# Copies of two PSUM banks at a time, and a small early zero write to the output, in a batched fp32-in, fp32-out matmul

## The chip, the cores and the metric

The kernel runs on one core of one Trainium2 chip. The metric is the device time of one execution in microseconds (us); a comparison is made between executions of the two kernels on the same chip.

## The reference

Sixteen independent products: for each batch, x (768 x 512) transposed times y (768 x 1024).

```python
def setup_inputs():
    batch, m, k, n = 16, 512, 768, 1024
    return {
        "x": np.random.randn(batch, k, m).astype(np.float32),
        "y": np.random.randn(batch, k, n).astype(np.float32),
    }

def reference(x, y):
    return np.einsum('bkm,bkn->bmn', x, y).astype(np.float32)
```

## The kernel before

Each batch loads x (1.5 MB) and y (3 MB) as fp32, casts them to bf16 on the vector engine (DVE), and runs 48 matmuls of 512 columns on the tensor engine (PE): 4 row blocks x 2 column halves x 6 steps of the contraction. The 6 steps accumulate in one bank of PSUM, the memory that PE writes its results to, so a batch has eight groups in eight banks. The scalar engine (ACT) copies each bank to SBUF, the memory that loads and stores use, and one store writes the 2 MB of the batch. All loads and stores are issued from one queue, the sync queue (SP in the profile), and the store of a batch stands four batches of loads behind it.

```python
    psum = ctx.enter_context(tc.tile_pool(name="psum", bufs=8, space=bass.MemoryType.PSUM))
    LAG = 4
    ...
        for b in range(B):
            ...
            load(xs[:], x_v[b], 1)
            for h in range(halves):                  # 2 in the last batch, else 1
                ks = slice(h * KT // halves, (h + 1) * KT // halves)
                load(ys[:, ks], y_v[b, :, ks], 1)
            if b >= LAG:
                store(b - LAG)
            ...                                      # casts x_sb<-xs, y_sb<-ys on DVE
            for h in range(halves):
                for mo in range(MT):
                    for nt in range(NT):
                        if h == 0:
                            ps[mo, nt] = psum.tile([P, NF], FP32, name="ps")
                        for kt in range(h * KT // halves, (h + 1) * KT // halves):
                            mm(ps[mo, nt], x_w, y_sb, kt, mo, nt)
                        if h == halves - 1:
                            nc.scalar.copy(o_sb[:, mo, nt * NF:(nt + 1) * NF], ps[mo, nt][:])
        for b in sorted(o_tiles):
            store(b)
```

## Time and profile before

| | before |
|---|---|
| time, median of the runs beside the first measurement of the change | 262.25 us (262.04 to 262.52, 4 runs) |
| span of the profiled execution | 260.5 us |
| packets of the sync queue, share of the 16 DMA engines' span | 98.4% |
| bytes read and written | 109.06 MB, at a mean of 419 GB/s |
| busy: PE / DVE / ACT | 73% / 32% / 29% |
| copies out of PSUM | 128 of 587 ns |

The row to start from is the third. DMA engines that are busy for 98.4% of the span leave at most the other 1.6%, some 4 us, to be won by other engines, at the start and at the end. The table also says what can cost time: whatever is added to the DMA engines. The lines themselves stand in the prediction below.

In the windows view, GB/s divided by the DMA share is the rate at which the DMA engines move data while they are busy. It is about 430 where all packets take their usual time (430 / 1.01 = 426 from 10 to 55 us before), and falls where packets take longer.

### The profile page before, as it was taken

The page shows a single profiled execution, that of the slowest core. Times are in us where ns is not written, and L with a number is a line of the kernel's source. Part 1 is how long each engine was busy: PE and PEld are TensorE (multiplying, and loading weights), DVE is VectorE, ACT ScalarE, POOL GpSimd, SP SyncE. Part 2 cuts the span into 40 slices and gives each one's busy share as a digit, 9 for nine tenths or more (in the row PEclk, how much of TensorE's full clock was granted, in tenths as well). Part 3 has the DMA queues.
Part 4 walks back from the last instruction along what each step waited for, and adds up shares of the span by engine and source line. Part 5 has one row for each costly group of instructions (what it writes and reads, how often), then busy time and mean ns, then how long its engine had stood idle before and what let it go on. Part 6 is the DMA issues. An engine that isn't in the chain of part 4 may idle for free.

```text
span 260.5 us, 1879 instructions
## 1 busy us (share of the span) xinstructions
PE 191.3 (73%) x768; PEld 89.3 (34%) x768; DVE 83.1 (32%) x48; ACT 76.4 (29%) x129; POOL 0.2 (0%) x4
## 2 busy tenths in 40 slices
PE   0049999897939959688496966969789395899600
PEld 0014555453513514334142432434335142355200
DVE  0271633525222252322524214252132522252000
ACT  1003444442421403324032330323314043141600
POOL 0000000000000000000000000000000000000000
PEclk9999999999985977979898896797979889799955
DMA  7999999999999999999999999999999999999994
GB/s 279 434 434 411 445 423 436 426 387 420 446 416 442 423 422 455 409 440 418 438 435 415 453 418 431 423 428 449 410 443 421 426 445 407 431 430 430 435 428 201
DMA packets 7065, 109.18 MB, mean 419 GB/s; under 512 B 784, under 2 KB 784, under 8 KB 784
## 3 DMA queue, kind: packets, MB, share of 16 engines
q1 hardware_dynamic: 7056, 109.06, 98.4%
q8 instruction: 6, 0.10, 0.1%
q14 instruction: 3, 0.02, 0.0%
HBM read 75.50 MB, written 33.55 MB: 419 GB/s over the span
## 4 chain that ended last, share of the span: by engine, by line
DMA 74%; DVE 11%; PE 8%; issue 0%; ACT 0%; SPq 0%; DVEq 0%
DMA ys<-in_y_dram 74%; DVE y_sb L78 11%; PE ps L56 8%; ACT o_sb L93 0%; SPq L50 0%; DVEq L78 0%
## 5 line engine op out<-in xcount | busy, mean ns | idle before, releaser
L56 PE MATMUL ps<-y_sb,x_sb 128*128 128x512 bf16 x768 | 191.3, 412 | 53.8 <-DVE y_sb L78 53.8
L56 PEld LDWEIGHTS <-x_sb 128*128 128x128 bf16 x768 | 89.3, 118 | 155.2 <-issue 45.9
L93 ACT COPY o_sb<-ps 128x512 f32<-128x512 f32 x128 | 75.1, 587 | 168.6 <-PE ps L56 168.2
L78 DVE CAST y_sb<-ys 128x3072 bf16<-128x3072 f32 x32 | 55.0, 1757 | 87.4 <-DMA ys<-in_y_dram 87.4
L75 DVE CAST x_sb<-xs 128x3072 bf16<-128x3072 f32 x16 | 28.2, 1760 | 66.6 <-DMA xs<-in_x_dram 60.4
L93 ACT ACT_TABLE_LOAD x1 | 1.3, 1283 | 0.7 <-PEq L110 0.7
L110 POOL MEMSET const-bfloat16-1.0<- 128x1 bf16 x1 | 0.1, 101 | 0.0
L110 POOL MEMSET const-uint8-127<- 128x1 uint8 x1 | 0.1, 101 | 0.0
L110 POOL MEMSET const-float32-0.0<- 128x1 f32 x1 | 0.1, 98 | 0.2 <-issue 0.2
L110 POOL MEMSET const-float32-1.0<- 128x1 f32 x1 | 0.1, 98 | 0.0
## 6 DMA issues: line engine op xcount, KB each, us to landing
ys<-in_y_dram SPq DMA_DIRECT2D x15, 3072.0 KB, 28.1
out_dram<-o_sb SPq DMA_DIRECT2D x16, 2048.0 KB, 32.6
xs<-in_x_dram SPq DMA_DIRECT2D x16, 1536.0 KB, 29.7
ys<-in_y_dram SPq DMA_DIRECT2D x2, 1536.0 KB, 26.1
```

What stands on the lines that cost most here:

```text
L56: nc.tensor.matmul(ps[:], x_w[:, kt, mo], y_sb[:, kt, nt * NF:(nt + 1) * NF], start=(kt == 0), stop=(kt == KT - 1))
L75: nc.vector.tensor_copy(x_sb[:], xs[:])
L78: nc.vector.tensor_copy(y_sb[:, ks], ys[:, ks])
L93: nc.scalar.copy(o_sb[:, mo, nt * NF:(nt + 1) * NF], ps[mo, nt][:])
L110: nc = _bacc.Bacc("TRN2", target_bir_lowering=False, num_devices=1)
```

## The change

Two things are changed. PSUM tiles become two banks wide, so that ACT copies 1,024 columns with one instruction in place of twice 512 and pays ACT's fixed cost of an instruction once in place of twice. And a tile of zeros, 128 rows of 512 B, is written to the first output batch on the sync queue just behind the first loads; the store of batch 0 overwrites it later. The write may have been meant to ready the output's memory or the queue before the first real store comes.

```diff
-    psum = ctx.enter_context(tc.tile_pool(name="psum", bufs=8, space=bass.MemoryType.PSUM))
+    psum = ctx.enter_context(tc.tile_pool(name="psum", bufs=4, space=bass.MemoryType.PSUM))
+    z_pool = ctx.enter_context(tc.tile_pool(name="z_pool", bufs=1))
 ...
+            if b == 0:
+                z = z_pool.tile([P, 128], FP32, name="z")
+                nc.vector.memset(z[:], 0.0)
+                nc.sync.dma_start(o_v[0, :, 0, 0:128], z[:])
             if b >= LAG:
                 store(b - LAG)
 ...
                 for mo in range(MT):
+                    if h == 0:
+                        ps[mo] = psum.tile([P, NT, NF], FP32, name="ps")
                     for nt in range(NT):
-                        if h == 0:
-                            ps[mo, nt] = psum.tile([P, NF], FP32, name="ps")
                         for kt in range(h * KT // halves, (h + 1) * KT // halves):
-                            mm(ps[mo, nt], x_w, y_sb, kt, mo, nt)
-                        if h == halves - 1:
-                            nc.scalar.copy(o_sb[:, mo, nt * NF:(nt + 1) * NF], ps[mo, nt][:])
+                            nc.tensor.matmul(
+                                ps[mo][:, nt], x_w[:, kt, mo],
+                                y_sb[:, kt, nt * NF:(nt + 1) * NF],
+                                start=(kt == 0), stop=(kt == KT - 1))
+                    if h == halves - 1:
+                        nc.scalar.copy(o_sb[:, mo].rearrange("p (t f) -> p t f", f=NF), ps[mo][:])
```

The rest of the diff writes the helpers load, store and mm out in line and changes nothing in the instructions.

More of the change, by code (lines that the diff above doesn't have):

```diff
@@ L47 @@
     o_tiles = {}
-    def load(dst, src, rows):
-        nc.sync.dma_start(dst, src)
     def store(b):
-        nc.sync.dma_start(o_v[b], o_tiles.pop(b)[:])
-    def mm(ps, x_w, y_sb, kt, mo, nt):
-        nc.tensor.matmul(ps[:], x_w[:, kt, mo], y_sb[:, kt, nt * NF:(nt + 1) * NF],
-                         start=(kt == 0), stop=(kt == KT - 1))
+        o_sb = o_tiles.pop(b)
+        nc.sync.dma_start(o_v[b], o_sb[:])
     with tc.manual_schedule():
@@ L64 @@
             halves = 2 if b == B - 1 else 1
-            load(xs[:], x_v[b], 1)
+            nc.sync.dma_start(xs[:], x_v[b])
             for h in range(halves):
                 ks = slice(h * KT // halves, (h + 1) * KT // halves)
-                load(ys[:, ks], y_v[b, :, ks], 1)
+                nc.sync.dma_start(ys[:, ks], y_v[b, :, ks])
+            if b == 0:
+                z = z_pool.tile([P, 128], FP32, name="z")
+                nc.vector.memset(z[:], 0.0)
+                nc.sync.dma_start(o_v[0, :, 0, 0:128], z[:])
             if b >= LAG:
```

## The prediction

> **What bounds the kernel now.** I read the page first, because its busy shares and its DMA row say which resource is full; then stretches of the windows view, to see when it is full; then the timeline of the DMA issues and of the end, to see how much room the other engines have.
>
> ```profile
> span 260.5 us, 1879 instructions
> ...
> PE 191.3 (73%) x768; PEld 89.3 (34%) x768; DVE 83.1 (32%) x48; ACT 76.4 (29%) x129; POOL 0.2 (0%) x4
> ...
> DMA  7999999999999999999999999999999999999994
> ...
> q1 hardware_dynamic: 7056, 109.06, 98.4%
> ...
> L93 ACT COPY o_sb<-ps 128x512 f32<-128x512 f32 x128 | 75.1, 587 | 168.6 <-PE ps L56 168.2
> ```
>
> The DMA row is at 9 in 38 of 40 slices, and the packets of the one queue fill 98.4% of the 16 engines' span: 0.984 x 260.5 = 256.3 us of packet time for each DMA engine, in a span of 260.5. No compute engine comes near: PE is busy for 73%, ACT for 29% with 168 us of waiting for PE. The chain of waits tells the same story (74% of the span is put down to the loads of y), but it ends in PE and a copy at 245.6 us and leaves out the last 15 us of stores, so I do not take the end from it.
>
> The windows view below gives window, its length, the busy time and count of each engine, then granted clock, DMA share and GB/s (a packet is counted where it starts).
>
> ```profile
> 0.00:3.00 3.00, 0.00 (x0) 0.00 (x0) 0.00 (x0) 1.28 (x1) 0.20 (x4) 1.00 0.41 82
> 3.00:10.00 7.00, 0.00 (x0) 0.11 (x1) 1.76 (x1) 0.00 (x0) 0.00 (x0) 1.00 1.04 446
> 10.00:55.00 45.00, 37.77 (x161) 18.61 (x161) 20.76 (x12) 15.27 (x26) 0.00 (x0) 1.00 1.01 430
> 55.00:61.00 6.00, 6.00 (x29) 3.17 (x28) 0.22 (x1) 2.70 (x5) 0.00 (x0) 1.00 0.99 381
> 61.00:235.00 174.00, 137.46 (x536) 62.39 (x534) 58.62 (x34) 52.14 (x90) 0.00 (x0) 0.87 1.01 429
> 235.00:256.00 21.00, 10.03 (x47) 5.02 (x45) 1.76 (x1) 4.99 (x9) 0.00 (x0) 0.80 1.01 430
> 256.00:260.50 4.50, 0.00 (x0) 0.00 (x0) 0.00 (x0) 0.00 (x0) 0.00 (x0) 0.50 0.24 102
> ```
>
> From 3 to 256 us the DMA engines run at about 430 GB/s, with one dip: 381 GB/s from 55 to 61 us. In the packet records of the trace the first 16 KB packets of a store start at 57.7 us, and just before that, from 55 to 58 us, 31 of the 24 KB load packets take about 1.2 us where the others take 912 ns; summed and divided by 16 engines that is about 0.63 us. The other losses are the start (82 GB/s in the first 3 us) and the ragged end (102 GB/s in the last 4.5 us, as the 16 engines do not finish together).
>
> How much room the compute side has at the end can be read from the timeline:
>
> ```profile
> 0.73 0.38 SPq L50 DMA_DIRECT2D xs<-in_x_dram  x1
> 1.17 0.42 SPq L50 DMA_DIRECT2D ys<-in_y_dram  x1
> 1.64 0.42 SPq L50 DMA_DIRECT2D xs<-in_x_dram  x1
> 2.10 0.68 SPq L50 DMA_DIRECT2D ys<-in_y_dram  x1
> ...
> 208.13 37.88 SPq L53 DMA_DIRECT2D out_dram<-o_sb  x5
> ```
>
> ```profile
> 223.11 21.92 PE L56 MATMUL ps<-y_sb,x_sb 128*128 128x512 bf16 x93 [0.83 <-DVE y_sb L78]
> ...
> 234.71 0.59 ACT L93 COPY o_sb<-ps 128x512 f32<-128x512 f32 x1 [0.71 <-PE ps L56]
> ...
> 240.58 5.07 ACT L93 COPY o_sb<-ps 128x512 f32<-128x512 f32 x8 [5.29 <-PE ps L56]
> ```
>
> The last store is issued by 208.13 + 37.88 = 246.0 us. After that moment the queue still moves about 10.0 x 0.430 + 4.5 x 0.102 = 4.76 MB, of which the last store is 2.10 MB. So 2.66 MB, or 2.66 / 0.430 = 6.2 us of work, stand in the queue ahead of it: the last store could be issued some 6 us later before a DMA engine runs dry.
>
> **What the Trainium skill says.** "DMA: Bandwidth & Descriptors", Specifications, puts the ceiling of the 16 DMA engines at 435 GB/s and 512 B as the smallest transfer at line rate. The trace agrees with the first (430, 429 and 430 GB/s in the three long windows, so some 1% is left). The zero write has rows of exactly 512 B, so it stands at the second limit; the kernel before has no such packet to compare. The same page, Queues, rings and completion order, says that each DMA engine takes the descriptors of a ring in order. The trace fits: x of batch 0 is cast from 7.1 us and y from 14.4 us, in the order of issue. So the zero write will start only after the first 4.72 MB. The same page, Bandwidth, Measured, gives 0.95 us of DMA time for a 64 KB transfer alone (on another issue path); I use it as a pessimistic size. "ScalarE: Activation LUTs", What ACT_TABLE_LOAD costs, gives an ACT instruction with immediate scale and bias 186 ns + 0.833 ns per element: 612 ns for 512 elements, where this trace has 587. I keep the slope and anchor it on the 587.
>
> **The change part by part.**
>
> Two-bank copies: 128 copies of 587 ns become 64 copies of 1,024 columns. Each is 587 + 512 x 0.833 = about 1,014 ns (an estimate). ACT: 64 x 1.014 = 64.9 us in place of 75.1, so 10.2 us less busy time. All of it lies beside DMA work, and ACT waits for PE anyway (168 us). Worth on the path: 0.
>
> PSUM buffers: 8 tiles of one bank become 4 of two, the same eight banks. In the dense part a one-bank copy comes every 0.59 + 0.71 = 1.30 us, which is 6 matmuls, so a two-bank tile takes PE 2.59 us. PE comes back to a tile after three others, 7.8 us; the copy is done 1.0 us after the last matmul. In the last batch's first half PE spends 1.30 us on a tile and reaches the fourth after 3.9 us, still longer than one copy. No new wait of PE. In its second half a tile takes 6 matmuls or 1.30 us against 1.01 us of copy, so ACT keeps up. The very last copy ends 1.01 us after PE instead of 0.58: the last store is issued about 0.4 us later, against 6.2 us of room. Worth: 0.
>
> Zero write, issue: one memset of 128 elements on DVE, idle until 7.12 us, and one more DMA issue of about 0.42 us on the sync queue. The order of instructions shows it third, after x and y of batch 0; it waits for DVE alone, and the memset should be over before the queue reaches it at about 1.64 us. x and y of batch 1 are issued 0.4 us later, at about 2.1 and 2.5 us, behind 4.72 MB or 11 us of queued loads. No gap.
>
> Zero write, transfer: 128 rows of 512 B, 8 on each DMA engine. The packet records have 4 B packets at 9 ns, 12 KB at 460, 24 KB at 912, which is 8 ns + bytes / 27.2 per ns; 512 B is then 27 ns, and 8 of them 0.22 us on each engine (an estimate). As the engines are full, this comes on the path whole: +0.2 us, up to 0.95 if such rows run as badly as the page's 64 KB case.
>
> First-store dip: if the 0.63 us at 55 to 58 us is the price of the first write to the output, the zero write may move it to about 12 us, where it costs the same, or spare it. I give a third to sparing: -0.2 us. The batch 0 store rewrites the same bytes much later and carries only its wait for ACT, so no new wait there.
>
> Sum: 0 + 0 + 0.2 - 0.2 = 0 us; **262.4 us**.
>
> **The rivals.** (a) The zero write pays the first-write price early and hides it: about -0.6 + 0.2 = -0.4 us, 262.0. For it: the dip stands beside the first store and has no twin of its size later (61 to 235 us holds 429). Against: the slow packets are loads that precede the first store, and a stall at 12 us finds the DMA engines just as full. (b) The small rows and an early turn from reading to writing stall the rings: +0.5 to +1 us, 263.1. For it: rows at the 512 B limit; against: mixed loads and stores run at 429, the same as loads alone at 430. (c) The coarser PSUM tiles make PE wait and the last store late. For it: half as many buffers; against: 6.2 us of room. It would need a delay of over 6 us to show at all, and 5 us more for 2%. (d) The ragged end shifts: the engines finish over about 3 us, and any change of the order of packets may move the slowest by some tenths either way. This is what I expect to set the sign.
>
> **Range and chances.** Faster by 2% means 257.2 or less, but the packets alone fill 256.3 us of each engine, and about 3 us of start and end come to it; all packets slower than their kind's usual time sum to only 2.2 us. Slower by 2% means 5.2 us more, over five times the pessimistic zero write. So same has 0.97. Inside that, the runs before spread over 0.5 us and rivals a, b and d move it by under 1 us: 261.5 to 263.3 us.
>
> **What would show it right or wrong.** Right: ACT has 64 copies of about 1.01 us and some 10 us less busy time; q1 has 144 more packets and 109.12 MB at 98% again; windows from 10 us on at 430 GB/s; the span within 1 us of 260.5. The zero write's part is right if DMA around 12 us loses no more than some tenths; rival (a) if the 55 to 61 us dip goes and nothing comes at 12 us; rival (b) if the GB/s fall there. The prediction would be wrong if the DMA row shows slices well below 9 in the middle or before the last store (then the last store came over 6 us late), or if the common rate over 61 to 235 us moves off 429.

## The result

| | before | changed |
|---|---|---|
| first comparison, median | 262.25 us (262.04 to 262.52, 4 runs) | 262.63 us (262.50 to 263.29, 4 runs) |
| ratio, 95% interval | | 1.0018 (1.0002 to 1.0033) |
| second comparison, median | 262.04 us (261.74 to 262.55, 9 runs) | 262.09 us (262.01 to 262.35, 5 runs) |
| ratio, 95% interval | | 1.0000 (0.9987 to 1.0014) |

Nothing that matters has changed. The first comparison put the change 0.4 us above the kernel before, the second (the run "whole" below) at no difference. The profiled execution of the first comparison, whose lines follow, was its slowest, 263.29 us.

The page of the changed kernel, the lines that answer to those in the prediction, and the row of the new transfer (the last number is the us from issue to landing):

```profile
span 261.4 us, 1817 instructions
...
DMA  7999999999999999999999999999999999999993
...
q1 hardware_dynamic: 7200, 109.12, 98.2%
...
L93 ACT COPY o_sb<-ps 128x1024 f32<-128x1024 f32 x64 | 64.9, 1014 | 180.0 <-PE ps L88 180.0
...
out_dram<-z SPq DMA_DIRECT2D x1, 64.0 KB, 13.2
```

ACT is busy for 10.2 us less, and its waiting for PE has grown from 168 to 180 us: what it saved, it waits. The DMA row is the same, with 144 more packets (128 rows and 16 that count the landing).

The windows of the changed kernel (window, length, busy us and count of PE, PEld, DVE, ACT, POOL, then clock, DMA share, GB/s):

```profile
10.00:15.00 5.00, 0.00 (x0) 0.00 (x0) 0.37 (x1) 0.00 (x0) 0.00 (x0) 1.00 0.95 401
...
55.00:61.00 6.00, 6.00 (x30) 3.13 (x29) 0.28 (x1) 2.33 (x3) 0.00 (x0) 1.00 0.96 373
61.00:235.00 174.00, 138.30 (x532) 62.30 (x531) 58.56 (x34) 44.63 (x44) 0.00 (x0) 0.86 1.01 430
235.00:256.00 21.00, 10.83 (x51) 5.44 (x48) 1.76 (x1) 5.07 (x5) 0.00 (x0) 0.89 1.01 430
```

and the one window of the kernel before that was not shown yet:

```profile
10.00:15.00 5.00, 0.00 (x0) 0.00 (x0) 0.59 (x1) 0.00 (x0) 0.00 (x0) 1.00 0.95 408
```

The two long windows run at 430 GB/s as before. Where the zero rows pass, from 10 to 15 us, 7 GB/s are missing for 5 us, 35 KB or less than 0.1 us of work (packets are counted where they start, so a tenth either way means nothing). The dip at 55 to 61 us, which the zero write might have removed, is there in full: 373 / 0.96 = 389 GB/s while busy, before 381 / 0.99 = 385.

The timeline of the changed kernel at the start (issues of the sync queue) and at the end (last copy, last stores):

```profile
1.17 0.42 SPq L63 DMA_DIRECT2D ys<-in_y_dram  x1
1.64 0.42 SPq L67 DMA_DIRECT2D out_dram<-z  x1
2.11 0.63 SPq L60 DMA_DIRECT2D xs<-in_x_dram  x1
...
208.94 38.30 SPq L53 DMA_DIRECT2D out_dram<-o_sb  x5
```

```profile
245.87 1.01 ACT L93 COPY o_sb<-ps 128x1024 f32<-128x1024 f32 x1 [0.28 <-PE ps L88]
```

The zero write takes 0.42 us of the sync queue and waits for nothing, and the second load of x is issued at 2.11 us, long before the DMA engines need it. The last copy ends at 246.9 us, the last store is issued by 247.2 us.

### The profile page after: what moved, and what is told of

Its sections match the earlier page's. It is cut to its first block, busy times and chain, and to the rows that moved or that the text cites. A ratio compares the mean times of both kernels' runs of the same rounds, so it can differ in the third digit from the quotient of the medians.

```text
span 261.4 us, 1817 instructions
## 1 busy us (share of the span) xinstructions
PE 192.8 (74%) x768; PEld 89.6 (34%) x768; DVE 83.3 (32%) x49; ACT 66.2 (25%) x65; POOL 0.2 (0%) x4
## 4 chain that ended last, share of the span: by engine, by line
DMA 74%; DVE 11%; PE 8%; ACT 0%; issue 0%; SPq 0%; DVEq 0%
DMA ys<-in_y_dram 74%; DVE y_sb L75 11%; PE ps L88 8%; ACT o_sb L93 0%; SPq L60 0%; DVEq L75 0%
## 5 line engine op out<-in xcount | busy, mean ns | idle before, releaser
L93 ACT COPY o_sb<-ps 128x1024 f32<-128x1024 f32 x64 | 64.9, 1014 | 180.0 <-PE ps L88 180.0
## 6 DMA issues: line engine op xcount, KB each, us to landing
out_dram<-z SPq DMA_DIRECT2D x1, 64.0 KB, 13.2
```

Of the source, the lines that this page charges most:

```text
L93: nc.scalar.copy(o_sb[:, mo].rearrange("p (t f) -> p t f", f=NF), ps[mo][:])
```

## The experiments

Ten kernels ran, all correct. They are told in the order of the questions. The changes are to the kernel before unless it says otherwise; the line that makes the pool of z is left out of the cuts. Where packet records are named, single packets of the trace were read: their size, start and duration, summed and divided by the 16 DMA engines.

### The two parts alone

**psum_only**: the changed kernel without the zero write.

```diff
-            if b == 0:
-                z = z_pool.tile([P, 128], FP32, name="z")
-                nc.vector.memset(z[:], 0.0)
-                nc.sync.dma_start(o_v[0, :, 0, 0:128], z[:])
```

> The two-bank copies alone, without the zero write. Theory (compute side is off the path): ACT 64 copies of about 1.014 us, 65 us busy, and the same time as before, ratio 1.000 within 0.001. Rival (coarser tiles delay the last store or stall PE, and this is what the 0.4 us of the change are): ratio 1.001 to 1.002, or 262.5 to 262.8 us, with PE waits on ACT in the list of waits.

Measured: 262.00 us, ratio 0.9997 (0.9984 to 1.0010). ACT has 64 copies of 1,014 ns, 64.9 us busy, and PE waits for ACT nowhere in the list of waits. The copies are worth nothing, as the theory has it. The interval ends at 1.0010, so the rival's 1.001 to 1.002 is not supported either.

**zero_only**: the kernel before with the zero write.

```diff
+            if b == 0:
+                z = z_pool.tile([P, 128], FP32, name="z")
+                nc.vector.memset(z[:], 0.0)
+                nc.sync.dma_start(o_v[0, :, 0, 0:128], z[:])
```

> The zero write alone, with the one-bank copies of before. Theory (the full DMA engines pay the 8 packets of 27 ns each, 0.22 us): before + 0.2 us, ratio 1.0008 (1.000 to 1.0016). Rival (the write also turns the queue round or waits for the output memory, which costs more than its packets): + 0.4 us or more, ratio 1.0015 or more, with slow load packets around 13 us. The dip at 55 to 58 us stays in both.

Measured: 262.16 us, ratio 1.0004 (0.9991 to 1.0016). This is in the range of the theory, but the interval reaches from a gain to 0.4 us, so alone it cannot tell 0.2 us from nothing. In the packet records of the trace every one of the 128 rows took 27 ns, and no load packet from 10 to 20 us took longer than usual (912 ns for 24 KB).

**zero8**: the zero write eight times as large, to make its price visible: 512 rows each into the first two output batches.

```diff
+            if b == 0:
+                z = z_pool.tile([P, MT, 128], FP32, name="z")
+                nc.vector.memset(z[:], 0.0)
+                for d in range(2):
+                    nc.sync.dma_start(o_v[d, :, :, 0:128], z[:])
```

> The zero write eight times as large: 1024 rows of 512 B in two issues, into the first two output batches. Theory (each 512 B row costs its 27 ns of packet time and nothing else): 64 packets per DMA engine, 1.73 us, so before + 1.7 us (ratio 1.0066, 263.9 to 264.3 us). If only bytes counted: 0.524 MB at 430 GB/s is 1.2 us (ratio 1.0046). If the cost were a fixed one for the first write: about +0.4 us as in the change (ratio 1.0015). The rows' packets should read 27 ns each.

Measured: 263.74 us, ratio 1.0064 (1.0051 to 1.0077), which is 0.0064 x 262.1 = 1.68 us, or 0.21 us for an eighth of it. The 64 rows on each DMA engine took 27 ns each, 1.73 us. The bytes alone (ratio 1.0046) lie outside the interval, and a fixed price (1.0015) lies far outside. (In us the median lies just under the range, 263.9 to 264.3, as the kernel before was faster in these rounds.) So the price of the small write, scaled down from the large one, is the packet time of its rows, about 0.2 us. What the expectation did not foresee is in the windows:

```profile
10.00:15.00 5.00, 0.00 (x0) 0.00 (x0) 0.00 (x0) 0.00 (x0) 0.00 (x0) 1.00 0.94 310
...
55.00:61.00 6.00, 5.44 (x26) 2.88 (x26) 2.27 (x2) 2.35 (x4) 0.00 (x0) 1.00 0.93 399
```

At 55 to 61 us the busy engines run at 399 / 0.93 = 429 GB/s: the dip is gone. It has come back at 10 to 15 us (310 / 0.94 = 330; the small rows alone account for a part of this). In the packet records, 34 load packets from 11 to 14 us were slow, 0.89 us per DMA engine in sum, and at 55 to 59 us all took their usual 0.92 us. So a larger early write does move the dip, and moving it gains nothing, because the engines are as full at 12 us as at 56 us.

**whole**: the changed kernel itself, with more rounds.

> The whole change again, with five rounds, because its first comparison has an interval from 1.0002 to 1.0033. Theory (the copies are worth nothing, the 8 rows cost 0.22 us): ratio 1.0008, interval down to 1.000 or just below. Rival (the two parts together cost more than each alone): ratio 1.0018 again.

Measured: 262.09 us, ratio 1.0000 (0.9987 to 1.0014). The 1.0018 of the first comparison did not come again. The expected 1.0008 lies in both intervals, which overlap from 1.0002 to 1.0014: the change costs some tenths of a us at most.

### What the dip is

**lag3**: the stores three batches behind the loads, so that the first store stands behind the fourth y and not the fifth.

```diff
-    LAG = 4
+    LAG = 3
```

> The kernel before with the stores three batches behind the loads in place of four, so that the first store stands behind y of batch 3. Question: what the slow load packets at 55 to 58 us are (0.6 us per DMA engine), which the zero write did not take away. If they belong to the first full store, they move to about 44 to 47 us and the stretch 55 to 61 us comes to 425 GB/s or more. If they belong to the time or to the loads of batch 4, they stay at 55 to 58 us. Total time: within 0.5 us of before, as bytes are the same and the queue stays full.

Measured: 262.39 us, ratio 1.0012 (0.9998 to 1.0025), unclear and small. The windows:

```profile
43.00:49.00 6.00, 6.00 (x30) 3.16 (x28) 0.00 (x0) 2.69 (x5) 0.00 (x0) 1.00 0.95 321
...
55.00:61.00 6.00, 6.00 (x30) 3.13 (x28) 1.76 (x1) 2.65 (x5) 0.00 (x0) 1.00 1.01 434
```

The dip has gone with the store: 321 / 0.95 = 338 GB/s while busy at 43 to 49 us, and nothing at 55 to 61 us. It belongs to the first full store, not to a time and not to the loads of batch 4. The slow packets are again loads, those of the 3 us just before the first packets of the store.

**zero4k**: the early write with rows of 4 KB, so that each DMA engine has eight packets as in the change, but 32 KB as in zero8.

```diff
+            if b == 0:
+                z = z_pool.tile([P, 1024], FP32, name="z")
+                nc.vector.memset(z[:], 0.0)
+                nc.sync.dma_start(o_v[0, :, 0, 0:1024], z[:])
```

> The zero write alone, with rows of 4096 B: still 8 packets on each DMA engine, but 32 KB of them in place of 4 KB. Question: what takes the slow load packets from 55 to 58 us to the early write, as the write of 64 rows of 512 B per engine did and that of 8 rows did not. If the bytes (32 KB per engine): slow load packets at 11 to 13 us, none at 55 to 58 us. If the number of write packets: they stay at 55 to 58 us. Time in both: 8 x (8 + 4096/27.2) ns = 1.27 us more than before, ratio 1.0049, 263.2 to 263.7 us.

Measured: 263.45 us, ratio 1.0050 (1.0036 to 1.0064), or 1.3 us, as expected from the packet time (most of the 4 KB rows took 159 ns).

```profile
10.00:15.00 5.00, 0.00 (x0) 0.00 (x0) 0.00 (x0) 0.00 (x0) 0.00 (x0) 1.00 0.92 315
...
55.00:61.00 6.00, 6.00 (x29) 3.13 (x28) 1.76 (x1) 2.44 (x5) 0.00 (x0) 1.00 0.95 408
```

The dip has moved to 10 to 15 us (315 / 0.92 = 342) and is gone at 55 to 61 us (408 / 0.95 = 429). The number of write packets is therefore not what matters: eight of 4 KB on an engine do it, eight of 512 B do not. What matters lies in the bytes, somewhere between 4 KB and 32 KB for each engine, or in how long the burst of writes lasts (0.2 or 1.3 us); this run does not tell the two apart, and zero_early below does so in part. No run shows why load packets slow down before the first burst of writes and before none of the later ones.

### Can an early write be hidden at the start?

The DMA engines are busy for only 0.41 of the first 3 us. This was the one place where a dip and the rows might cost nothing.

**zero_early**: the write of zero8, issued from the ACT queue ahead of everything else.

```diff
+            if b == 0:
+                z = z_pool.tile([P, MT, 128], FP32, name="z")
+                nc.vector.memset(z[:], 0.0)
+                for d in range(2):
+                    nc.scalar.dma_start(o_v[d, :, :, 0:128], z[:])
             load(xs[:], x_v[b], 1)
```

> The eight-fold zero write (64 rows of 512 B per engine) issued from the ACT queue at the very start, so that its rows and the once-only stall of the first large write could fall into the first 3 us, where the DMA engines are busy for 0.41 of the time. If both hide there: no slow load packets at 55 to 58 us or at 11 to 13 us, 0.6 to 0.9 us saved, and at most a few tenths paid: 261.3 to 262.0 us (ratio 0.997 to 0.9995), faster than both kernels. If the rows are merely paid in full, in turns with those of x: 1.73 us more, less the stall, 262.8 to 263.9 us.

Measured: 268.11 us, ratio 1.0233 (1.0218 to 1.0248), slower by 6 us. Neither expectation was near. The second queue of the page, the list of what the sync queue waited for (us in total, times, longest), and two windows:

```profile
q10 hardware_dynamic: 1056, 0.52, 0.7%
```

```profile
SPq L51 <- DMA out_dram<-z: 27.9, 2, 20.4
```

```profile
46.00:52.00 6.00, 5.08 (x25) 2.46 (x23) 1.89 (x2) 2.79 (x5) 0.00 (x0) 1.00 0.43 137
...
60.00:64.00 4.00, 3.46 (x17) 1.59 (x14) 0.00 (x0) 1.88 (x4) 0.00 (x0) 1.00 1.04 303
```

The sync queue waited twice for the zero write to land, 20.4 us the longer time, and the DMA engines ran dry: 137 GB/s from 46 to 52 us. The write landed only 48 us after its issue. The packet records show the cause: from 10 to 40 us they hold 755 rows of the write and 688 load packets, about one row (1.1) for each load packet. A load of x has 8 packets of 460 ns per engine, one of y 8 of 912 ns, 0.69 us in the mean; at one row of 27 ns for each, 64 rows take 64 x 0.71 = 46 us, and the records have the first row at 5.5 and the last at 49.5 us. The load waits because the two kinds of transfer share a set of eight completion semaphores: in the order of instructions, the load of x in batch 4 waits for the semaphore of the second zero write before it may use it again. The program does the same in all variants; only here had the earlier holder not landed.

The second window bears on the dip. By 50 us each engine had written 32 KB, as much as in zero8 and zero4k, but row by row between loads. The dip came all the same, just before the first packets of the first full store (63.9 us): 303 / 1.04 = 291 GB/s while busy, 34 slow load packets, 1.35 us per engine. So bytes written before do not suffice to bring the dip forward; it seems that they have to come in one burst. This is one trace, after a stretch in which the engines had run dry, so it points that way and does not settle it.

**zero4k_early**: to test this explanation, eight rows of 4 KB per engine from the ACT queue.

```diff
+            if b == 0:
+                z = z_pool.tile([P, 1024], FP32, name="z")
+                nc.vector.memset(z[:], 0.0)
+                nc.scalar.dma_start(o_v[0, :, 0, 0:1024], z[:])
             load(xs[:], x_v[b], 1)
```

> The write of eight 4096 B rows per DMA engine, issued from the ACT queue at the start. Two questions. First, why the eight-fold write from the ACT queue cost 6 us: theory, its 64 rows per engine take turns with the load packets one by one, so it lands only after 48 us and a load waits for its landing; with 8 rows it must land by about 10 us and no load waits, so there is no hole at 46 to 52 us. Rival: a second queue itself slows the engines, and the time stays near 268 us. Second, whether the once-only stall and the bytes can hide in the first 3 us: if so 261.5 to 262.3 us, if not 263.2 to 263.7 us as from the sync queue.

Measured: 263.22 us, ratio 1.0039 (1.0027 to 1.0052). The write lands 13.8 us after its issue (later than the 10 us expected; its first row starts only at 5.8 us), no load waits for it, and there is no hole. So a second queue does not by itself cost the six us of zero_early. Nor were they the late landing alone: the profiled span of zero_early is 5.9 us longer than that of before, and by the packet records 3.0 us of this are idle time of the DMA engines, 1.8 us the packet time of the rows and 1.1 us slower load packets. On the second question the answer is no: 1.0 us more than before, against 1.3 us for the same write from the sync queue, is still a loss.

```profile
3.00:10.00 7.00, 0.00 (x0) 0.11 (x1) 1.76 (x1) 0.68 (x1) 0.00 (x0) 1.00 1.04 417
...
55.00:61.00 6.00, 6.00 (x29) 3.18 (x28) 0.73 (x1) 2.51 (x5) 0.00 (x0) 1.00 0.98 382
```

The packet records have slow load packets at both places here, 0.41 us per engine at 3 to 8 us and 0.49 us at 56 to 59 us; its eight rows per engine were spread over 5.8 to 15.1 us, between a burst and the row by row of zero_early. No variant of the early write beat the kernel before.

### How much room the compute side has

The prediction rests on the last store having some us of room. Two kernels use it up on purpose; they are the changed kernel with every copy done two and three times.

**copy2** and **copy3** (here 3):

```diff
-                        nc.scalar.copy(o_sb[:, mo].rearrange("p (t f) -> p t f", f=NF), ps[mo][:])
+                        for _ in range(3):
+                            nc.scalar.copy(o_sb[:, mo].rearrange("p (t f) -> p t f", f=NF), ps[mo][:])
```

> The changed kernel with every copy out of PSUM done twice. Theory (the last store may be issued some 5 us later before a DMA engine runs dry; in the profile of the changed kernel 4.3 MB are still to move after its issue at 247.2 us, 2.2 MB of them ahead of it, 5.2 us): ACT busy 130 us, the last copy ends at about 250 us and the last store is issued some 3.5 us later, and the time is that of the change, 262.3 to 262.9 us, ratio under 1.003. Rival (the chain of PE and copies sets the end): 3.5 us longer, 266 us.

Measured for copy2: 262.31 us, ratio 1.0008 (0.9993 to 1.0023). ACT is busy for 129.4 us in copies, twice as long, and the last store is issued by 249.2 us; the time is that of the change. The chain of PE and copies does not set the end.

> The changed kernel with every copy out of PSUM done three times. Same theory: the last copy ends at about 254 us, the last store is issued some 7.4 us later than in the change, 2.2 us more than the room of 5.2 us, so 264 to 266 us (ratio 1.008 to 1.014), with a hole in the DMA row just before the last store. If the chain of copies set the end: 7.4 us longer, 270 us. If there were no limit to the room: 262.6 us.

Measured for copy3: 262.77 us, ratio 1.0032 (1.0010 to 1.0054), 0.8 us more than before. This missed: at least 1.008 was expected. The last copies and the last stores in the timeline, then two windows:

```profile
241.55 12.11 ACT L94 COPY o_sb<-ps 128x1024 f32<-128x1024 f32 x12 [2.84 <-PE ps L88]
...
207.90 46.12 SPq L53 DMA_DIRECT2D out_dram<-o_sb  x5
```

```profile
252.00:254.00 2.00, 0.00 (x0) 0.00 (x0) 0.00 (x0) 1.63 (x2) 0.00 (x0) 0.50 0.40 172
...
258.00:260.00 2.00, 0.00 (x0) 0.00 (x0) 0.00 (x0) 0.00 (x0) 0.00 (x0) 0.50 0.62 262
```

The same windows of the changed kernel:

```profile
252.00:254.00 2.00, 0.00 (x0) 0.00 (x0) 0.00 (x0) 0.00 (x0) 0.00 (x0) 0.50 1.01 434
...
258.00:260.00 2.00, 0.00 (x0) 0.00 (x0) 0.00 (x0) 0.00 (x0) 0.00 (x0) 0.50 0.14 57
```

and the last stores of whole:

```profile
207.80 38.31 SPq L53 DMA_DIRECT2D out_dram<-o_sb  x5
```

The hole that the theory asks for is there: the last store was issued by 207.90 + 46.12 = 254.0 us, and from 252 to 254 us the engines are busy for 0.40 only. The time alone would not show a limit, as 262.6 us, the value for a room without one, lies in the interval; the hole and the end do. The end is no longer ragged. By the last 4 B packet of each engine (the one that counts the landing) the 16 engines finish the last store within 0.2 us of each other, at 259.4 to 259.6 us; in the run whole they finish over 2.9 us, from 256.0 to 258.9 us. The working of the expectation took the mean over 16 engines, where the slowest one counts. In whole that one ends at 258.9 us and needs 8 x 0.611 = 4.9 us for its part of the last store, so it is free for it at 254.0 us. The packets of the store start 0.5 us after its issue (254.0 to 254.5 us in copy3), so it has to be issued by 253.5 us; whole issues it by 246.1 us, and the room is 7.4 us. copy3 issues it 7.9 us later, 0.5 us over the limit, and its slowest engine ends 0.7 us later. The faster engines stand idle meanwhile, which costs nothing.

## Why the prediction was right

The time on record was 262.4 us with a range from 261.5 to 263.3; the first comparison measured 262.63 and the second 262.09 us. Step by step:

- **The bound.** Right. The long windows run at 430 GB/s before and after, the DMA row is full in both, and the one kernel that took 6 us more (zero_early) is the one that let the DMA engines run dry.
- **Copies of two banks.** Right in size and in worth: 1,014 ns were estimated and measured, ACT's busy time in copies fell by 75.1 - 64.9 = 10.2 us, and psum_only stands at 0.9997. The slope taken from "ScalarE: Activation LUTs" in the Trainium skill, 0.833 ns per element, is confirmed by the two sizes: (1,014 - 587) / 512 = 0.834.
- **PSUM tiles.** Right. PE waits for ACT nowhere in psum_only, so rival (c) falls. In the profiled changed kernel the last copy ends at 246.9 us against 245.6 us before, and most of that is the profiled run's own lateness: in whole the last store is issued by 246.1 us, against 246.0 us before.
- **Room at the end.** Right that it is ample, shown by copy2. The 6.2 us were worked out from the mean over the engines; by the slowest engine it is 7.4 us, with the 0.5 us from issue to first packet taken off. An error to the safe side here, but the same working spoiled the expectation for copy3.
- **The zero write's issue.** Right: 0.42 us of the queue, no wait, no gap.
- **The zero write's transfer.** Right: rows of 27 ns, 0.22 us on each engine. zero8 makes it 0.21 us for an eighth of the large write; no run of the small write itself can tell 0.2 us from nothing. The 0.95 us of the pessimistic rival (b) did not appear.
- **The dip.** The step "I give a third to sparing: -0.2 us" failed: the term was 0. The dip stayed where it was in the changed kernel, neither moved nor spared. It does belong to the first large burst of writes (lag3, zero8, zero4k), so the suspicion was sound, but a write of 4 KB for each engine is too small to bring it forward, and one of 32 KB moves it without gain. The sum should have been +0.2 us, 262.6 us. Rival (a) falls with it. So small a term could not have been told from noise in the result: whole shows no difference at all, and that the sum on record fits it better than +0.2 us would is luck.
- **The ragged end**, which was "what I expect to set the sign": the traces bear this out from run to run. The slowest engine ends at 259.3 us in the profiled kernel before, at 260.1 us in the changed one and at 258.9 us in whole, and the spans follow it (260.5, 261.4, 260.2 us), while the mean end of the 16 engines stays at 257.3, 257.6 and 257.4 us. So most of the 0.9 us by which the profiled changed kernel was longer is its slowest engine. As whole is the same kernel and was shorter than before, nothing shows that the change moves it.

Of the skill's other places: the 435 GB/s of "DMA: Bandwidth & Descriptors", Specifications, agree with the 430 of the windows. That an engine takes the descriptors of a ring in order (Queues, rings and completion order) agrees with the zero write landing 13.2 us after its issue, behind the first loads. The same section says that an engine takes turns between queues, at packet granularity, and zero_early agrees: about one row for each load packet, and 48 us for 64 rows.

Left open: why loads slow down before the first large burst of writes and not before later ones, and what size or length of burst sets it off (between 4 and 32 KB for each engine). The first loads of all are slow too: in the kernel before, 16 packets of 12 KB in the first 3 us took 1.1 us in the mean in place of 0.46, 0.66 us per engine, as much as the dip. No run looked into it.

## What to carry to other kernels

Where the packets of the DMA queues fill the span, as here, saving instructions elsewhere was worth nothing as long as the last store kept its room, and added packets were paid in full (1.7 us for 1.73 us of them), so price a change by its packets. A one-time stall is not removed by bringing it forward to a moment at which the same engines are just as full. Small rows on a second queue take turns with the large packets of the first, so they land late; look which later transfer waits for their semaphore before putting them there.

## What the Trainium skill lacked or had wrong

- "DMA: Bandwidth & Descriptors", Specifications, gives 512 B as the smallest transfer at line rate. In a full queue a 512 B row took 27 ns here, 19 B per ns and engine, against 26.8 for 16 KB (611 ns) and 25.8 for 4 KB (159 ns): at 512 B a queue is at about 70% of its rate.
- The same page, Bandwidth, Measured, gives 0.95 us for a 64 KB transfer. That is a load, alone and on another issue path, so the page is not wrong, but it does not say what such a transfer adds: for a store behind others in a full queue it cost 0.2 us (1.68 us for eight times as much).
- The same page, Queues, rings and completion order, speaks of 9 to 17 descriptors that an engine drains from one queue before it turns to another. In zero_early the turns were about one row of 512 B against one load packet (755 to 688 from 10 to 40 us): 64 rows took 48 us.
- No page has the once-only stall before the first large burst of writes: 0.6 to 1.2 us per DMA engine in the runs with one queue, in load packets (24 KB in 1.2 to 1.5 us in the mean in place of 0.912).
- No page gives a figure for how far apart the 16 engines finish a long stream: 2.9 us after some 250 us in whole, 3.4 us in the kernel before, which makes the slowest engine, not the mean, the measure of the room before a last store.
- "ScalarE: Activation LUTs", What ACT_TABLE_LOAD costs, has 186 ns + 0.833 ns per element, 612 and 1,039 ns; measured from PSUM to SBUF were 587 and 1,014 ns. The slope fits; for this copy the fixed part is 25 ns too high.
